# Gated branch of the mixer by pairs of feature tiles, with recurrent gates and scans moved forward

## The chip, the cores and the metric

The kernel runs on one core of a Trainium2 chip. The metric is the device time of one execution in microseconds (us), as a median over runs. The engines are named as in the profile: PE is TensorE's matmul, PEld its weight load, DVE is VectorE, ACT is ScalarE, POOL is GpSimd, SP is SyncE, which issues the loads. Only ACT and DVE take matmul results out of PSUM; POOL works on SBUF alone here.

## The reference, cut to what matters

One layer over 512 tokens of 1024 features: a gated feed-forward net (1024 to 2816 and back), a mixer, and a second feed-forward net, each between root-mean-square norms. The mixer is what the change touches:

```
u = rms_norm(h, mix_pre_g)
q, k, v, xr, xg = split(u @ w_in)              # xr, xg: 1024 features each
xr = causal_conv(xr, conv_w, conv_b)           # 4 taps along the tokens
r  = sigmoid(blockdiag(xr, wa) + ba);  ig = sigmoid(blockdiag(xr, wx) + bx)
a  = exp(-8 r softplus(-lambda));      b  = sqrt(1 - a*a) * ig * xr
hr[t] = a[t]*hr[t-1] + b[t]                    # scan along the tokens
y_a = (hr * gelu(xg)) @ w_lru_out              # the gated branch
y_b = attention(q, k, v) @ w_attn_out
merged = sigmoid(u@wgA + bA) * y_a + sigmoid(u@wgB + bB) * y_b
h = h + rms_norm(merged @ w_o, mix_post_g)
```

All of it is in float32.

## The kernel before

**Split matmuls.** Every operand of a matmul is a pair: `hi`, the value rounded to the fast matmul type, and `lo`, the rest. ACT writes `hi` by a copy and DVE writes `lo` by a subtraction (`split2`, L191, and `split_to`, L151). A product is three matmuls: hi·hi, lo·hi and hi·lo. The activations `u` lie transposed (features on partitions) in `uT`, `hi` and `lo` for 8 feature tiles of 128 by 512 tokens. A *unit* (`unit`, L209; `mm_feat`, L196) makes one output feature tile of 128 by 512 tokens: 8 feature tiles deep, three matmuls of 512 columns each, so 24 matmuls.

**Pairs.** In the feed-forward nets, `Pairs` (L477) makes two output feature tiles at a time by seven block products for eight (the Winograd form of Strassen's method). The weights of two tiles are cut in four blocks, the activations in four blocks of (4 feature tiles) x (256 tokens). Weight sums S1 to S4 and activation sums T1 to T4 are formed first; a product (`mm_s`, L465) is 4 feature tiles deep, three matmuls of 256 columns each, so 12 matmuls, and some of the products accumulate on another's PSUM bank after ACT has copied a partial result out (`q1`, `q5`, `u`, `v`). `prep(m, i)` (L492) prepares the weights of job m in five steps: 0 forms the sums (on POOL in the second net), 1 splits the first raw tile, 2 splits S1 and S2, 3 splits S3 and S4, 4 splits the last block. Its order of products is a11, s1, (a22 of the job before), s2, a12, s4, s3; so ACT's copy of a11's result must come before s2 accumulates on the same bank.

**Order of the work.** The order on each engine is that of the program text; there is no scheduler. `order` (L102 to L132) lists the weight tiles in the order of use, `get` (L163) issues loads and splits a few tiles ahead, and `split_to` stops at tiles that are marked `paired`. `later(n, fn, rank)` (L177) defers work by n *points*; a unit has two points (after each half), a token tile of `wv` and a product of a pair have one. At a point, work that is due is put out in order of rank; `point(True)` puts out all that is left. A deferred step lands in the engines' queues at its point, and an engine that is ahead may do it earlier in time, an engine that is behind later.

**The mixer's projections.** `tok_gemm` (L333) ends the first net: the last 7 feature tiles are taken token tile by token tile, each token tile is normed, transposed by PE into PSUM and copied to `uT` (`transpose_out`, L317). With `xf` given, `transpose_xf` (L327) copies each transposed bank a second time, unrounded, to four tiles of SBUF; the second net's call has that (for T1 to T4 there), the first net's call, L888, has it not. Then come the units, 8 of `xr` (the first four inside `tok_gemm`), 8 of `wg`, 2 of `wk`, 4 token tiles of `wv`, 2 of `wq`, and 8 of `xg`. Counted from the end of `tok_gemm`, `xr` 4 to 7 take points 1 to 8, `wg` 9 to 24, `wk` 25 to 28, `wv` 29 to 32, `wq` 33 to 36, `xg` 37 to 52.

**The recurrent branch** rides along on points: `conv` (L914), `rg_gates` (L924; with `products`, 24 half-height matmuls for two tiles, and `gates`, four tanh on ACT each), `rg_decay` (L965; exp and tanh), `rg_scan` (L978; sqrt on ACT, then after a lag a product and the scan on DVE). The points stand in `CONV_AT`, `RG_AT`, `DECAY_AT`, `SCAN_AT`, `SCAN_LAG` (L1276 to L1284). The scan writes over the tile that held the convolved `xr`, one of 8 that live until `y_out` (L1070), which takes gelu of an `xg` unit, multiplies by the scan and splits the result.

**After it** come the 8 units of `lru` (over the 8 tiles `y`), mixed with the rest of `wq`, `wg` and the steps of attention (L1188 to L1214).

**Slots.** Nearly all SBUF tiles come from one pool of 42 slots of 4 KB per partition (`NSLOT`). A tile's first writer, a load, ACT, DVE or POOL, waits until the last reader of the slot's previous tile is done. PSUM has 8 banks, handled the same way.

Of the kernel before, what the change touches and what calls it, by code (L numbers as in the profile page):

```python
# [51 lines left out]
def hybrid_layer(ctx: ExitStack, tc: tile.TileContext, a: dict, out: bass.AP):  # L52
    nc = tc.nc
    act, dve, pool, pe, sp = nc.scalar, nc.vector, nc.gpsimd, nc.tensor, nc.sync
# [20 lines left out]
    def f32(ap):  # L75
        return ap.bitcast(F32)
# [9 lines left out]
    veps = cp.tile([P, NT], F32, name="veps")  # L86
# [15 lines left out]
    order = []  # L102
# [4 lines left out]
    paired = set()  # L107
# [26 lines left out]
    st = {"dma": 0, "split": 0, "get": 0}  # L134
# [42 lines left out]
    def later(n, fn, rank=1):  # L177
        uid[0] += 1
        due.append((now[0] + n, rank, uid[0], fn))
# [11 lines left out]
    def split2(hi, lo, src):  # L191

        act.activation(hi, src, AF.Copy)  # L193
        dve.tensor_tensor(out=lo, in0=src, in1=f32(hi), op=ALU.subtract)  # L194

    def mm_feat(ps, w, c0=0, c1=SEQ, xh=None, xl=None):  # L196

        wh, wl = w
        for k in range(KT):
            s = slice(k * P, (k + 1) * P)  # L200
            h_ = uT[:, 0, k, c0:c1] if xh is None else xh[k][:, c0:c1]
            l_ = uT[:, 1, k, c0:c1] if xl is None else xl[k][:, c0:c1]
            pe.matmul(ps[:, c0:c1], wh[:, s], h_, start=k == 0, stop=False)  # L203
            pe.matmul(ps[:, c0:c1], wl[:, s], h_, start=False, stop=False)  # L204
            pe.matmul(ps[:, c0:c1], wh[:, s], l_, start=False, stop=k == KT - 1)  # L205
# [231 lines left out]
    class Hidden:  # L437


        def __init__(self):  # L440
            self.f, self.t, self.done = [], {}, 0
# [35 lines left out]
    class Pairs:  # L477

        def __init__(self, na, nb, f0, X, hid, R=None):
            self.R = R
            self.jobs = [(nm, f) for f in range(f0, FT, 2) for nm in (na, nb)]
            self.na, self.X, self.hid = na, X, hid
            self.k0 = order.index((na, f0))
            self.w, self.c1, self.ready = {}, {}, set()

        def raws(self, m):
# [52 lines left out]
        def run(self, tail, hooks={}):  # L541
# [75 lines left out]

            last()

# [43 lines left out]
    hid, X1 = Hidden(), {}  # L663
    hid.f = [None] * NC1
    Rb = slot([P, 2, SEQ], name="Rb")
    pairs_a = Pairs("w1a", "w3a", NC1, X1, hid, Rb)
    h_load([a["x"][t * P : (t + 1) * P, :] for t in range(NT)])
    dma_to(NS + 3)
    dma_one(pairs_a.k0)
# [4 lines left out]
    ps = [bank("f") for _ in range(NS)]  # L674
# [23 lines left out]
    xg, tg = {(hh, th): slot([P, 4, 256], name="xg") for hh in range(2) for th in range(2)}, {}  # L698
# [17 lines left out]
    s4 = small(NT, "s4")  # L716
# [165 lines left out]
    X1 = pairs_a = late = None  # L882
# [4 lines left out]
    bs = tok_gemm("w2a", hid, FT, RF, "ffn1_post_g", 0.5, "mix_pre_g", [("xr", i) for i in range(4)], hid.to, spill=True, eps=veps)  # L887
    hid = None  # L888


# [87 lines left out]
    def rg_scan(i):  # L978
        s0, s1 = lru[i]
        t, ig, a_ = s0[:, 1, :], s1[:, 0, :], s1[:, 1, :]  # L980

        act.activation(t, t, AF.Sqrt, scale=0.25)

        def scan():
            dve.tensor_tensor(out=ig, in0=t, in1=ig, op=ALU.mult)
            dve.tensor_tensor_scan(t, a_, ig, 0.0, op0=ALU.mult, op1=ALU.add)
            lru[i] = s0

        later(SCAN_LAG[i], scan, 3)


    lru = {}
# [19 lines left out]
    for i in range(8):  # L1012
        ps = unit("wg", i)
# [16 lines left out]
    for i in range(2):  # L1030
        ps = unit("wk", i)
# [8 lines left out]
    for t in range(NT):  # L1040
        ps = bank("v")
        c = slice(t * P, (t + 1) * P)
# [21 lines left out]
    for i in range(2):  # L1064
        ps = unit("wq", i)
        later(1, lambda i=i, ps=ps: q_out(i, ps))

    ys = []

    def y_out(i, ps):  # L1070
        t = slot([P, 2, SEQ], name="ge")
        act.activation(t[:, 0, :], ps, AF.Gelu_apprx_tanh)
        dve.tensor_tensor(out=t[:, 1, :], in0=t[:, 0, :], in1=lru.pop(i)[:, 1, :], op=ALU.mult)
        y = slot([P, 2, SEQ], F32R, name="y")
        split2(y[:, 0, :], y[:, 1, :], t[:, 1, :])
        ys.append(y)
# [124 lines left out]
    for nm, i in att_units:  # L1201
        if nm == "lru":
            w = get(nm, i) if i else w_lru
            ps = bank("f")
            mm_feat(ps, w, xh=[y[:, 0, :] for y in ys], xl=[y[:, 1, :] for y in ys])
            later(1, lambda i=i, ps=ps: ya_out(i, ps))
            if i == 7:
                ys.clear()
# [21 lines left out]

    hid, tn = Hidden(), []
    X2 = {"b11": uview(0, 0), "b21": uview(1, 0), "b22": uview(1, 1)}
    pairs_b = Pairs("w1b", "w3b", NC2, X2, hid)
    dma_one(pairs_b.k0)
    dma_one(pairs_b.k0 + 1)
    for i, at_ in enumerate((2, 5, 7, 9, 11)):
# [1 line left out]
    for i in range(8):  # L1238
        if i:
            w = get("wao", i)  # L1240
        ps = bank("f")
# [4 lines left out]
    xf = {(hh, th): slot([P, 4, 256], name="xf") for hh in range(2) for th in range(2)}  # L1246
    def operands():
# [24 lines left out]
    X2 = pairs_b = None  # L1272
# [13 lines left out]
RF = 7  # L1286
RO = 6

NC1 = 4

NG = 2
NC2 = 2
# [54 lines left out]
```

## Time and profile before

| what | value |
|---|---|
| median of 3 runs | 1132.8 us (1132.72 to 1133.06) |
| profiled execution | 1132.6 us, its span 1130.8 us |
| granted TensorE clock | 0.998 |
| PE busy | 1122.6 us (99% of the span) |
| PEld, DVE, ACT, POOL busy | 1006.0, 797.2, 599.5, 303.8 us |
| bytes moved | 124.95 MB, mean 110 GB/s |

The span reaches from the first to the last instruction. A matmul's recorded time is longer than its distance to the next one, since matmuls overlap; the distance from start to start is what one costs. A wait for several things is put down to the one that came last.

### The profile page before, as it was taken

Reading aid. Unit: us, or ns where it says so; the run is one execution under the profiler, and the core shown is the slowest. Engines: PE = TensorE matmul, PEld = TensorE weight load, DVE = VectorE, ACT = ScalarE, POOL = GpSimd, SP = SyncE. Lnnn points to the kernel's source line nnn. Section 1 sums busy time; section 2 is a strip of 40 time slices with the busy share of each in tenths; the row PEclk is TensorE's granted clock in tenths of the full one; section 3 lists DMA queues with packets and bytes.
Section 4 is the critical chain, followed back from the end, with each engine's and each line's share of the span. In section 5 each row is a group of like instructions: output and inputs, shape, how many; then the busy total and the mean of one; then the engine's idle time right before and its main releaser. Section 6 shows DMA issues by size and latency. Waiting matters only on the chain.

```text
span 1130.8 us, 17501 instructions
## 1 busy us (share of the span) xinstructions
PE 1122.6 (99%) x6829; PEld 1006.0 (89%) x6829; DVE 797.2 (70%) x1219; ACT 599.5 (53%) x1065; POOL 303.8 (27%) x243
## 2 busy tenths in 40 slices
PE   9999999999999999999999999999999999999997
PEld 7899999988889887888888888889999999998886
DVE  5889989886446747695778855667898777975313
ACT  7755555574335359844656653356555555573211
POOL 0044444200000000001655642000965566700000
PEclk9999999999999999999999999999999999999999
DMA  9226563265314312134232333521332332254101
GB/s 343 88 95 148 133 131 112 76 223 168 102 59 152 119 54 71 60 111 132 60 90 76 94 118 99 184 104 39 112 95 94 112 112 79 90 199 173 39 19 56
DMA packets 37138, 124.95 MB, mean 110 GB/s; under 512 B 4528, under 2 KB 6448, under 8 KB 37056
## 3 DMA queue, kind: packets, MB, share of 16 engines
q1 hardware_dynamic: 34128, 114.89, 30.2%
q0 software_dynamic: 2640, 8.43, 3.7%
q8 instruction: 53, 0.87, 0.3%
q10 hardware_dynamic: 288, 0.52, 0.1%
q14 instruction: 29, 0.24, 0.1%
HBM read 116.50 MB, written 7.33 MB: 110 GB/s over the span
## 4 chain that ended last, share of the span: by engine, by line
PE 97%; ACT 2%; DVE 1%; issue 0%; DVEq 0%
PE c L472 11%; PE c L473 11%; PE c L474 11%; PE f L203 10%; PE f L204 10%; PE f L205 10%; PE acc L223 8%; PE acc L221 8%; PE acc L222 8%; PE pt L1148 1%; PE s L1112 1%; PE s L1111 1%; PE tr L313 1%; PE o L1164 1%; PE o L1165 1%; PE f L693 1%
## 5 line engine op out<-in xcount | busy, mean ns | idle before, releaser
L203 PE MATMUL f<-uT,whi 128*128 128x512 f32 (+1 forms) x472 | 171.6, 364 | 0.0
L204 PE MATMUL f<-uT,wlo 128*128 128x512 f32 (+1 forms) x472 | 170.3, 361 | 0.1
L205 PE MATMUL f<-uT,whi 128*128 128x512 f32 (+1 forms) x472 | 170.1, 360 | 0.0
L221 PE MATMUL acc<-whi,hT 128*128 128x512 f32 x352 | 137.1, 390 | 0.0
L222 PE MATMUL acc<-wlo,hT 128*128 128x512 f32 x352 | 137.0, 389 | 0.0
L223 PE MATMUL acc<-whi,hT 128*128 128x512 f32 x352 | 136.9, 389 | 0.0
L472 PE MATMUL c<-Xh,whi 128*128 128x256 f32 x456 | 129.1, 283 | 0.0
L474 PE MATMUL c<-Xl,whi 128*128 128x256 f32 x456 | 129.1, 283 | 0.0
L473 PE MATMUL c<-uT,wlo 128*128 128x256 f32 x456 | 129.0, 283 | 0.0
L473 PE MATMUL c<-Xh,wlo 128*128 128x256 f32 x456 | 129.0, 283 | 0.0
L474 PE MATMUL c<-uT,whi 128*128 128x256 f32 x456 | 129.0, 283 | 0.0
L472 PE MATMUL c<-uT,whi 128*128 128x256 f32 x456 | 129.0, 283 | 0.0
L194 DVE TENSOR_TENSOR wlo<-S,whi 128x1024 fp32r<-128x1024 f32 x76 | 113.7, 1496 | 2.0 <-ACT whi L193 1.1
L203 PEld LDWEIGHTS f<-uT,whi 128*128 128x128 f32 x472 | 89.1, 189 | 14.5 <-issue 1.4
L204 PEld LDWEIGHTS f<-uT,wlo 128*128 128x128 f32 x472 | 89.2, 189 | 13.5 <-DVE wlo L159 0.5
L205 PEld LDWEIGHTS f<-uT,whi 128*128 128x128 f32 x472 | 89.1, 189 | 13.5
L193 ACT ACTIVATE whi<-S 128x1024 fp32r<-128x1024 f32 x76 | 77.9, 1055 | 19.8 <-DVE S L518 19.8
L472 PEld LDWEIGHTS c<-Xh,whi 128*128 128x128 f32 x456 | 87.5, 192 | 0.3 <-issue 0.3
L472 PEld LDWEIGHTS c<-uT,whi 128*128 128x128 f32 x456 | 87.5, 192 | 0.0
L473 PEld LDWEIGHTS c<-uT,wlo 128*128 128x128 f32 x456 | 87.5, 192 | 0.0
L474 PEld LDWEIGHTS c<-uT,whi 128*128 128x128 f32 x456 | 87.5, 192 | 0.0
L473 PEld LDWEIGHTS c<-Xh,wlo 128*128 128x128 f32 x456 | 87.5, 192 | 0.0
(324 smaller groups left out, 2705.2 us busy)
## 6 DMA issues: line engine op xcount, KB each, us to landing
raw_w2a<-in_w2a_dram SPq DMA_DIRECT2D x22, 512.0 KB, 4.3
raw_w1b<-in_w1b_dram SPq DMA_DIRECT2D x22, 512.0 KB, 4.2
raw_w3b<-in_w3b_dram SPq DMA_DIRECT2D x22, 512.0 KB, 4.1
raw_w2b<-in_w2b_dram SPq DMA_DIRECT2D x22, 512.0 KB, 4.2
raw_w3a<-in_w3a_dram SPq DMA_DIRECT2D x21, 512.0 KB, 4.5
raw_w1a<-in_w1a_dram SPq DMA_DIRECT2D x20, 512.0 KB, 4.3
raw_wg<-in_wg_dram SPq DMA_DIRECT2D x16, 512.0 KB, 3.8
raw_xr<-in_xr_dram SPq DMA_DIRECT2D x8, 512.0 KB, 4.0
```

The costliest lines, as they stand in the source:

```text
L193: act.activation(hi, src, AF.Copy)
L194: dve.tensor_tensor(out=lo, in0=src, in1=f32(hi), op=ALU.subtract)
L203: pe.matmul(ps[:, c0:c1], wh[:, s], h_, start=k == 0, stop=False)
L204: pe.matmul(ps[:, c0:c1], wl[:, s], h_, start=False, stop=False)
L205: pe.matmul(ps[:, c0:c1], wh[:, s], l_, start=False, stop=k == KT - 1)
L221: pe.matmul(acc[n], x[:, 0, c], wh[:, s], start=first, stop=False)
L222: pe.matmul(acc[n], x[:, 0, c], wl[:, s], start=False, stop=False)
L223: pe.matmul(acc[n], x[:, 1, c], wh[:, s], start=False, stop=last)
L313: pe.transpose(ps[:, k * P : (k + 1) * P], hg[:, kk * P : (kk + 1) * P], ident)
L472: pe.matmul(ps, wh[:, s], xh, start=first, stop=False, skip_group_check=True)
L473: pe.matmul(ps, wl[:, s], xh, start=False, stop=False, skip_group_check=True)
L474: pe.matmul(ps, wh[:, s], xl, start=False, stop=k == 3, skip_group_check=True)
```

## The change

The eight `xg` units are replaced by four jobs of a new class `GeluPairs`, derived from `Pairs` (whose constructor now takes the names and an end). Each job makes two feature tiles by seven products of 12 matmuls; gelu, the product with the scan (`mult`) and the split of the result (`parts`) are done for two tiles at once, one job later. The last job's are done at the end, in pieces.

The activation sums T1 to T4 are needed for the mixer's `u` now: `xf` is given to the first net's `tok_gemm`, POOL does four subtractions in place on these tiles, and each is split to two slots at points 4, 5, 7 and 9 (`T_AT`). The first job's weight sums and splits are put at points 27, 30, 32, 33 and 34 (`PREP_AT`), the second job's sums, on POOL, at 34. The `xg` tiles are marked `paired`, so that `split_to` leaves them alone.

Gates move from points 7 to 23 to points 4 to 18, decays from 15 to 28 to points 10 to 23, the square roots from 29 to 32 to points 26 to 29, and the lags of the scans shrink, so that the last scan stands at point 34 and not 42. The scans write to four tiles of their own (two scans in each).

```diff
@@ order
+    paired.update(range(len(order), len(order) + 8))
     order += [("xg", i) for i in range(8)]
@@ after class Pairs
+    class GeluPairs(Pairs):
+        def run(self, scans, yh, yl, tail):
...
+            for n, (nm, f) in enumerate(self.jobs):
+                W = self.w.pop(n)
+                tmp = slot([P, 4, 256], name="ct")
+                q1, q5, u, v = (tmp[:, i, :] for i in range(4))
+                c = slot([P, 2, SEQ], name="cc")
+                bu, bx, bc = (bank("c")[:, :256] for _ in range(3))
+                mm_s(W["a11"], X["b11"], bu)
+                act.activation(q1, bu, AF.Copy)
+                mm_s(W["s1"], X["t1"], bx)
+                act.activation(q5, bx, AF.Copy)
+                self.prep(n + 1, 1)
+                last()
+                mm_s(W["s2"], X["t2"], bu, True)
+                act.activation(u, bu, AF.Copy)
+                mult()
+                self.prep(n + 1, 2)
+                mm_s(W["a12"], X["b21"], bc)
+                dve.tensor_tensor(out=c[:, 0, :256], in0=bc, in1=q1, op=ALU.add)
+                mm_s(W["s4"], X["b22"], bx, True)
+                dve.tensor_tensor(out=c[:, 0, 256:], in0=bx, in1=u, op=ALU.add)
+                parts()
+                self.prep(n + 1, 3)
+                if n == end:
+                    tail()
+                mm_s(W["s3"], X["t3"], bu, True)
+                act.activation(v, bu, AF.Copy)
+                dve.tensor_tensor(out=c[:, 1, 256:], in0=v, in1=q5, op=ALU.add)
+                gelu(c[:, 0, :])
+                if n < end:
+                    self.prep(n + 1, 4)
+                    self.prep(n + 2, 0)
+                self.raws(n + 3)
+                def last(W=W, bu=bu, c=c):
+                    mm_s(W["a22"], X["t4"], bu, True)
+                    act.activation(c[:, 1, :256], bu, AF.Gelu_apprx_tanh)
+                    gelu(c[:, 1, 256:])
+                def mult(c=c, sc=scans[f // 2]):
+                    dve.tensor_tensor(out=c, in0=c, in1=sc, op=ALU.mult)
+                def parts(c=c):
+                    yh.append(slot([P, 2, SEQ], F32R, name="yh"))
+                    yl.append(slot([P, 2, SEQ], F32R, name="yl"))
+                    split2(yh[-1], yl[-1], c)
+            # after the loop: mult, gelu and split of the last job in pieces, tail(), its a22
...
@@ first net's tok_gemm
+    xf = {(hh, th): slot([P, 4, 256], name="xf") for hh in range(2) for th in range(2)}
-    bs = tok_gemm("w2a", hid, FT, RF, ..., hid.to, spill=True, eps=veps)
+    bs = tok_gemm("w2a", hid, FT, RF, ..., hid.to, xf=xf, spill=True, eps=veps)
@@ rg_scan
-            dve.tensor_tensor_scan(t, a_, ig, 0.0, op0=ALU.mult, op1=ALU.add)
-            lru[i] = s0
+            if i % 2 == 0:
+                scans.append(slot([P, 2, SEQ], name="scan"))
+            dve.tensor_tensor_scan(scans[i // 2][:, i % 2, :], a_, ig, 0.0, op0=ALU.mult, op1=ALU.add)
@@ before the laters of conv, gates, decays, scans
+    pairs_g = GeluPairs(("xg",), 0, 8, X3)
+    for o_, p_, q_ in (((0, 0), (0, 1), (0, 0)), ((0, 1), (1, 1), (0, 1)), ((1, 1), (1, 1), (0, 0)), ((1, 0), (1, 0), (1, 1))):
+        pool.tensor_tensor(out=xf[o_], in0=xf[p_], in1=xf[q_], op=ALU.subtract)
+    for n, (key, o_) in enumerate((("t1", (0, 0)), ("t3", (0, 1)), ("t2", (1, 1)), ("t4", (1, 0)))):
+        later(T_AT[n], lambda key=key, o_=o_: X3.update({key: to_slots(xf.pop(o_))}), 3)
+    for i, p in enumerate(PREP_AT):
+        later(p, lambda i=i: pairs_g.prep(0, i), 3)
+    later(PREP_AT[-1], lambda: pairs_g.prep(1, 0), 3)
@@ after the units of wq
-    for i in range(8):
-        ps = unit("xg", i)
-        later(1, lambda i=i, ps=ps: y_out(i, ps))
+    yh, yl = [], []
+    point(True)
+    pairs_g.run(scans, yh, yl, lambda: split_to(st["split"] + 1))
@@ constants
-RG_AT = (7, 11, 13, 15, 17, 19, 21, 23)
+RG_AT = (4, 6, 8, 10, 12, 14, 16, 18)
-DECAY_AT = (15, 16, 19, 20, 23, 24, 27, 28)
-SCAN_AT = (29, 29, 30, 30, 31, 31, 32, 32)
-SCAN_LAG = (1, 2, 2, 4, 5, 7, 8, 10)
+DECAY_AT = (10, 11, 14, 15, 18, 19, 22, 23)
+SCAN_AT = (26, 26, 27, 27, 28, 28, 29, 29)
+SCAN_LAG = (1, 2, 2, 3, 3, 4, 4, 5)
+T_AT = (4, 5, 7, 9)
+PREP_AT = (27, 30, 32, 33, 34)
```

More of the change, by code (lines that the diff above doesn't have):

```diff
@@ L618, in run @@
             last()
+    class GeluPairs(Pairs):
+        def run(self, scans, yh, yl, tail):
+            X, end = self.X, len(self.jobs) - 1
+            assert st["get"] == st["split"] == self.k0, (st, self.k0)
+            st["get"] = st["split"] = self.k0 + 2 * len(self.jobs)
+            last = mult = parts = lambda: None
+            gelu = lambda v: act.activation(v, v, AF.Gelu_apprx_tanh)
+            for n, (nm, f) in enumerate(self.jobs):
[40 more added lines that the diff above has]
+                    split2(yh[-1], yl[-1], c)
+            sc, h_, l_ = scans[-1], slot([P, 2, SEQ], F32R, name="yh"), slot([P, 2, SEQ], F32R, name="yl")
+            dve.tensor_tensor(out=c[:, 0, :], in0=c[:, 0, :], in1=sc[:, 0, :], op=ALU.mult)
+            gelu(c[:, 1, 256:])
+            dve.tensor_tensor(out=c[:, 1, 256:], in0=c[:, 1, 256:], in1=sc[:, 1, 256:], op=ALU.mult)
+            split2(h_[:, 0, :], l_[:, 0, :], c[:, 0, :])
+            tail()
+            mm_s(W["a22"], X["t4"], bu, True)
+            act.activation(c[:, 1, :256], bu, AF.Gelu_apprx_tanh)
+            dve.tensor_tensor(out=c[:, 1, :256], in0=c[:, 1, :256], in1=sc[:, 1, :256], op=ALU.mult)
+            split2(h_[:, 1, :], l_[:, 1, :], c[:, 1, :])
+            yh.append(h_)
+            yl.append(l_)
@@ L886, in hybrid_layer @@
     later(10, softplus)
-    bs = tok_gemm("w2a", hid, FT, RF, "ffn1_post_g", 0.5, "mix_pre_g", [("xr", i) for i in range(4)], hid.to, spill=True, eps=veps)
+    xf = {(hh, th): slot([P, 4, 256], name="xf") for hh in range(2) for th in range(2)}
+    bs = tok_gemm(
+        "w2a", hid, FT, RF, "ffn1_post_g", 0.5, "mix_pre_g", [("xr", i) for i in range(4)], hid.to, xf=xf, spill=True, eps=veps)
     hid = None
@@ L1066, in hybrid_layer @@
         later(1, lambda i=i, ps=ps: q_out(i, ps))
[L1068 to L1076, printed above, removed]
-    for i in range(8):
-        ps = unit("xg", i)
-        later(1, lambda i=i, ps=ps: y_out(i, ps))
+    yh, yl = [], []
+    point(True)
+    pairs_g.run(scans, yh, yl, lambda: split_to(st["split"] + 1))
+    X3 = pairs_g = None
     def ya_out(i, ps):
```

19 lines of the change are left out of this document (9 added, 10 removed).

## The prediction

> **What bounds the kernel now.** I read the page's busy times first, then the chain of work that ended last, then PE's own rows where the change sits.
>
> ```profile
> PE 1122.6 (99%) x6829; PEld 1006.0 (89%) x6829; DVE 797.2 (70%) x1219; ACT 599.5 (53%) x1065; POOL 303.8 (27%) x243
> PE 97%; ACT 2%; DVE 1%; issue 0%; DVEq 0%
> 478.38 0.39 PE L205 MATMUL f<-uT,whi 128*128 128x512 f32 x1
> 483.82 0.39 PE L205 MATMUL f<-uT,whi 128*128 128x512 f32 x1
> 484.73 0.39 PE L203 MATMUL f<-uT,whi 128*128 128x512 f32 x1
> 485.19 0.50 PE L204 MATMUL f<-uT,wlo 128*128 128x512 f32 x1
> 528.61 0.39 PE L203 MATMUL f<-y,whi 128*128 128x512 f32 x1
> 82.87 0.28 PE L472 MATMUL c<-Xh,w 128*128 128x256 f32 x1
> 84.31 0.28 PE L472 MATMUL c<-Xh,whi 128*128 128x256 f32 x1
> ```
>
> PE is 97% of the chain, so time is won only by fewer or cheaper matmuls, and lost wherever PE comes to wait. The two rows at 478.38 and 483.82 are 24 matmuls apart: 226.7 ns each at 512 columns. Those at 82.87 and 84.31 are 12 apart, one product of a pair: 120.0 ns each at 256 columns. A line through both is 13.3 ns per matmul plus 0.417 ns per column, so halving a matmul doesn't halve its cost. The eight `xg` units begin at 484.73 and the first `lru` matmul is at 528.61: 43.88 us, of which 192 x 0.2267 = 43.52 is matmuls; most of the other 0.36 is the wait before 485.19 (0.23 beyond the usual distance).
>
> The gain rests on ACT and DVE keeping up, so next comes the busy time by stretch (PE, PEld, DVE, ACT, POOL, clock, DMA).
>
> ```profile
> 326.00:376.00 50.00, 50.00 (x317) 45.32 (x317) 36.37 (x74) 24.18 (x54) 2.77 (x4) 1.00 0.40 147
> 752.00:802.00 50.00, 50.00 (x326) 45.70 (x326) 36.86 (x72) 31.00 (x67) 10.69 (x5) 1.00 0.13 43
> 380.00:390.00 10.00, 10.00 (x45) 8.26 (x44) 6.00 (x8) 1.60 (x3) 0.00 (x0) 1.00 0.19 54
> 430.00:440.00 10.00, 10.00 (x46) 8.05 (x46) 6.70 (x11) 9.78 (x14) 0.00 (x0) 1.00 0.26 86
> 470.00:480.00 10.00, 10.00 (x62) 8.93 (x61) 7.21 (x12) 9.07 (x18) 0.00 (x0) 1.00 0.17 52
> 485.00:529.00 44.00, 43.93 (x194) 36.30 (x194) 33.16 (x39) 18.32 (x26) 4.87 (x10) 1.00 0.42 132
> 820.00:1000.00 180.00, 180.00 (x1502) 180.00 (x1501) 145.21 (x153) 96.40 (x171) 108.14 (x64) 1.00 0.31 101
> ```
>
> ACT is nearly full from 430 to 480 and idle before 390. The last row is the second net's pairs: 180 us at PE 180.00, with POOL forming the weight sums and DVE at 81%.
>
> **The change, part by part.**
>
> *PE.* Removed: 192 x 0.2267 = 43.52 us plus the 0.36. Added: 4 jobs x 7 products x 12 = 336 matmuls x 0.1200 = 40.32. Net -3.56 us if PE never waits. An eighth of 43.52 would be 5.44; the 144 extra matmuls take 1.92 of it back (144 x 13.3 ns).
>
> [...]
>
> *Second copies in the first net's `tok_gemm`, sums T on POOL, their splits.* Prices:
>
> ```profile
> L330 ACT ACTIVATE xf<-tr x8: 578/609/649, 767.9 to 790.4; 128x512 f32<-128x512 f32 x8
> L1251 DVE TENSOR_TENSOR T<-xf,xf x1: 1224/1224/1224, 790.6 to 790.6; 128x1024 f32<-128x1024 f32 x1
> L1253 DVE TENSOR_TENSOR T<-xf,T x1: 2311/2311/2311, 795.1 to 795.1; 128x1024 f32<-128x1024 f32 x1
> 791.16 2.95 POOL L1255 TENSOR_TENSOR T<-xf,xf 128x1024 f32<-128x1024 f32 x1 [49.65 <-ACT xf L330]
> 800.90 2.28 POOL L518 TENSOR_TENSOR S<-raw_w3b,raw_w3b 128x512 f32<-128x512 f32 x1
> 906.85 1.92 DVE L194 TENSOR_TENSOR wlo<-raw_w3b,whi 128x1024 fp32r<-128x1024 f32 x1
> 366.32 2.36 DVE L159 TENSOR_TENSOR wlo<-raw_xr,whi 128x1024 fp32r<-128x1024 f32 x2
> ```
>
> Eight copies x 0.61 = 4.9 us of ACT, four behind the last transposes (2.4 us). The second net's call runs with them (752 to 802) at PE 50.00 and ACT 31.0; the first's stage has ACT at 24.2. Cost 0; without that cover 2.4. Then 4 x 2.95 = 11.8 us of POOL, from about 367 to 379. A DVE subtraction of two SBUF tiles takes 1.22 us alone and 2.31 beside POOL's sum (L1251, L1253), so the four subtractions from 366.32 on end some 4 us later, before 375; the first weights are wanted at 378.9. Cost 0. Four splits at points 4 to 9, 4 x 1.05 of ACT and 4 x 1.22 of DVE, fall into the stretch with ACT at 1.6 of 10. The last one stands ahead of `conv(7)`, which feeds the gates' products at point 12: I count about 0.5 us to spare there, so 0 to 0.5 of waiting; 0 taken, since three of the four splits are long done.
>
> *Gates, decays, roots.* The same instructions, earlier. PE's 24 half-height matmuls per pair of tiles stay; ACT's full stretch (one round of 12.7 us: 8 tanh, 4 of the decays, 2 gates, 2 splits) starts four or five points sooner. Cost 0 by itself; what it buys is ACT time before the pairs: its work after the last decay (eight roots, `wk` and `wv` outputs, splits, `wq`) adds up to about 25 us, an estimate, with 31 to do it in.
>
> *DVE up to the second job.* This is the tight place. Rows:
>
> ```profile
> L986 DVE TENSOR_TENSOR_SCAN xc_t<-ig_e x8: 1224/1224/1226, 478.4 to 504.7; 128x512 f32<-128x512 f32 x8
> L985 DVE TENSOR_TENSOR ig_e<-xc_t,ig_e 128x512 f32<-128x512 f32 x8 | 5.5, 685 | 0.0
> L1061 DVE SCALAR_TENSOR_TENSOR QS<-f,QS 64x512 fp32r<-64x512 f32 x16 | 11.0, 688 | 0.5 <-ACT QS L1059 0.3
> 452.50 0.42 PE r L956
> 458.35 0.68 ACT ig_e L940
> 464.55 0.82 ACT ig_e L968
> 462.45 0.69 DVE KS L1024
> 477.39 0.43 DVE V L194
> 476.44 0.43 DVE L974 TENSOR_SCALAR ig_e<-ig_e 128x512 f32<-128x512 f32 x1
> 504.72 1.23 DVE L986 TENSOR_TENSOR_SCAN xc_t<-ig_e 128x512 f32<-128x512 f32 x1
> 483.93 1.21 DVE wlo L159
> ```
>
> Today the last scan ends at 506, 21 us into the `xg` units; the change queues all eight ahead of the pairs. The last gates' products go from 452.5 to about 439 (5 points of 2.72), their tanh end at 445 instead of 459, and after two decays of 1.64, two splits and two gates on ACT the last factors on DVE end at about 454 instead of 477 (an estimate). From there DVE owes, before the second job's first weights are whole: 8 scans x 1.91 = 15.3; `lo` of `wv` and `wq` 4.9; `wk`, `wv` and `wq` outputs 2.8 + 1.7 + 2.8; first job's preparation 3 x 1.22 + 0.68 = 4.3; the second's first `lo` 1.2. Sum 33.0, so 487. Beside it POOL forms 8 weight sums of up to 2.28 (17 to 18 us), and next to POOL such a subtraction takes 1.92 rather than 1.22 (906.85): up to 6.5 us lost, which gives 493.5; waits on `wk` and `wv` can add 2. The second job starts six products after 484.73, at 493.4. So 0 to 2.1 us of waiting. I take 0.5: the last row shows the present stage already entering with a DVE backlog of this kind, and PE lost only about 0.3 to it.
>
> *Inside the jobs.* In the second net a job of 10.08 us costs DVE 8.1 (145.21 over 17.9 jobs) and ACT 5.4. Here the multiplication by the scan and the residual of two tiles, 1.22 each as L1251, come on top, and the second net's own product and silu (about 1 and 0.7 us a job) go, for gelu and a split on ACT (1.4 + 1.05): DVE about 9.6, ACT about 7.2, estimates. That holds for two of the four jobs; the first has nothing to multiply, the last nothing to prepare. ACT's copy of a11's result must be done 1.44 us later in the first job (2.88 later on); ACT enters idle by my count. Gelu waits for DVE's sums and stands ahead of that copy, so a DVE more than 1.5 us later than above would be felt a second time. 0 taken.
>
> *Exit.* After the last product ACT and DVE owe the last two tiles some 6 us (gelu, multiplication, two splits, two splits of `lru` and `wq` weights); the seventh and eighth tile are wanted 4.1 us after the end plus 0.9 of attention scores, that is 6.4 after s3. Cost 0 to 1; 0 taken. Step 0 of attention starts about 2 us later on DVE and has room:
>
> ```profile
> 537.21 3.17 POOL L1132 TENSOR_SCALAR P<-P,d 128x128 f32<-128x128 f32 x4 [7.42 <-ACT es L1126]
> 545.10 0.60 PE L1148 MATMUL pt<-ident,P 128*128 128x128 f32 x4
> ```
>
> POOL is done at 540.4 and PE asks at 545.1.
>
> *Loads.* The same bytes, no new ones; the `xg` loads sit at the same place of SP's queue, apart from tiles 2 and 3, now behind the slots that the scans free.
>
> *Sum.* -3.56 + 0.5 = -3.1 on the profiled 1132.6, so 1129.5; the median stands 0.2 above that execution: **1129.7 us**.
>
> **The rivals.**
>
> *The gain is eaten at the entry (no change).* The DVE backlog or a late copy stops PE for 1.3 to 5.8 us in the first two jobs. For it: the sum above ends within 0.1 us of its deadline at POOL's full interference. Against it: PE 180.00 of 180 in the second net with the same interference. Time 1130.5 to 1135.1.
>
> *Slots starve the second job (slower).* By the program text, point 27 has all 42 slots taken (4 `wg`, 2 of `wk`, 8 of T, 16 of the recurrent branch, 6 split weights, 4 raw tiles, 2 sums), while the stage today holds about 31 there. The raw tiles of the second job then wait for the scans:
>
> ```profile
> SPq L143 <- DVE xc_t L986: 25.2, 4, 9.9
> DMA to landing us min/median/max: 3.4/3.7/4.4
> 518.19 2.18 POOL L1093 DMA_DIRECT2D BT<-bias_scr  x4 [163.86 <-PE f L205]
> ```
>
> Four of SP's loads already wait for scans, and POOL's load for attention waits for a slot until 518. If the last raw tile is issued at 489, it lands at 493, S1 and S2 take POOL 4.5, the split 3: 500, wanted at 494.8, and ACT, held at S3 and S4, delays the copies PE waits for. That is 5 to 9 us, so 1134 to 1138. It decides when that tile lands after about 493.3: then the stop passes 5.8 us, which is 3.56 plus 0.2% of the time. Against it: a scan every 2 us frees two slots.
>
> [...]
>
> *A full eighth.* If 256 columns cost half of 512, 1127.5. The rows at 82.87 and 84.31 exclude it.
>
> **How the numbers follow.** 0.2% (2.3 us) is about what a measurement of this kernel can tell from no change. Gain mostly kept, 1129.0 to 1130.5: 0.52, the forecast. Eaten at the entry: 0.28. Slots 0.17 and exclusion 0.02: slower, 0.19 together. Full eighth 0.01, below the range. The gain is little above the bound, so faster is 0.53 only, same 0.28, slower 0.19. The range runs from 1129.0 (no wait at all is 1129.2, less the spread) to 1136.0, which leaves out the upper part of the slot rival (0.10), exclusion and the full eighth. The likeliest case's own range is 1129.0 to 1130.5.
>
> **What the new profile would show.** Right: PE rows of `c` at 120 ns from about 484.7, the first `lru` matmul 40.3 to 41 us later, no idle PE above 0.3 us before 484.7; the last scan on DVE before 490; DVE about full from 455 to 515. Wrong: PE waiting for `wlo` at the second job (entry), SP's load of `xg` 2 or 3 after 488 or POOL's sums of the second job ending after 497 (slots), DVE subtractions of 3 us and more (exclusion), PE waiting at the gates' products or at the first `xr` units (the moved steps), or on `yl` in `lru` (exit).

## The result, and the profile after

| kernel | median | against the kernel before (95% interval) | span of the profiled execution |
|---|---|---|---|
| before | 1132.74 us | | 1130.8 us |
| changed | 1140.97 us | 1.0076 [1.0063, 1.0089] | 1138.8 us |

Each kernel ran six times: 1132.6 to 1133.1 us before, 1140.5 to 1142.7 us changed. The change makes the kernel 8.2 us slower; the forecast was 3.1 us faster. In the two traces the whole difference lies in the branch's own stage. From its first matmul to the first one of `lru` it took 43.88 us; now the stage goes from 484.38 to 536.38, 52.00 us, although its matmuls are 336 x 0.120 = 40.32. So PE stood still or ran slowly for 11.7 us.

The changed kernel's page (first line and busy times), then PE's rows behind its waits, in order of time (start, duration, line, operation; in brackets the idle time and what ended it):

```profile
span 1138.8 us, 17875 instructions
PE 1122.6 (99%) x6973; PEld 1012.7 (89%) x6973; DVE 831.6 (73%) x1238; ACT 618.9 (54%) x1102; POOL 345.2 (30%) x263
```

```profile
487.13 0.28 PE L475 MATMUL c<-Xl,whi 128*128 128x256 f32 x1
490.79 0.58 PE L473 MATMUL c<-Xh,whi 128*128 128x256 f32 x1 [3.38 <-ACT ct L637]
...
499.05 0.39 PE L474 MATMUL c<-uT,wlo 128*128 128x256 f32 x1 [0.68 <-DVE wlo L195]
...
513.37 0.39 PE L474 MATMUL c<-Xh,wlo 128*128 128x256 f32 x1 [2.54 <-DVE wlo L195]
...
518.29 0.39 PE L473 MATMUL c<-Xh,whi 128*128 128x256 f32 x1 [0.60 <-ACT ct L637]
...
534.85 0.38 PE L473 MATMUL c<-Xh,w 128*128 128x256 f32 x1 [0.47 <-ACT ct L655]
```

Measured from start to start beyond the usual 0.12, the five waits are 3.54, 0.83, 2.70, 0.90 and 0.63 us: ACT's copy `q1` of the first job, the first weights of the second, S1 of the third, `q1` of the third, and ACT's copy `v` ahead of the last product. That is 8.6. Another 2.7 are two stretches of matmuls at about 0.21 us instead of 0.12, from 490.8 and from 514.7 on (the first is shown at the end of this document), and 0.4 are slower first matmuls after a wait (0.22 or 0.23 us to the next). Before 484 PE waits nowhere, as forecast.

The busy time by stretch (PE, PEld, DVE, ACT, POOL, each with its number of instructions, then granted clock, DMA share, GB/s) shows who was late:

```profile
440.00:460.00 20.00, 20.00 (x90) 16.52 (x89) 10.31 (x14) 17.16 (x25) 0.00 (x0) 1.00 0.34 106
460.00:470.00 10.00, 10.00 (x78) 9.65 (x77) 9.90 (x7) 5.96 (x10) 6.71 (x4) 1.00 0.10 16
480.00:490.00 10.00, 7.41 (x45) 6.42 (x43) 9.93 (x9) 4.06 (x6) 6.18 (x4) 1.00 0.20 55
490.00:500.00 10.00, 8.54 (x57) 8.34 (x58) 9.76 (x11) 5.69 (x8) 1.38 (x1) 0.83 0.00 2
```

DVE is full from 480 to 500 and half idle from 440 to 460. ACT, named at the longest wait, is busy 4.06 of 10 there. Its own rows tell what held it:

```profile
486.51 1.20 ACT L1143 ACTIVATE QS<-f 64x512 fp32r<-64x512 f32 x2 [3.71 <-DVE scan L1060]
488.68 1.20 ACT L1143 ACTIVATE QS<-f 64x512 fp32r<-64x512 f32 x2 [0.97 <-DVE wlo L195]
490.35 0.38 ACT L637 ACTIVATE ct<-c 128x256 f32<-128x256 f32 x1 [0.47 <-DVE ig_e L1057]
```

Three instructions in a row need a fresh slot (`QS`, `QS`, `ct`), and each waits until DVE has let one go: by a scan, by a split, by the product ahead of a scan. The `q1` copy that PE asks for stands behind them. So the question becomes why DVE is late. Two things are in its rows. First its idle time, while scans whose square roots were done (the first two at 454.4, inside the first of these gaps) stood behind other work in its queue:

```profile
455.40 1.23 DVE L160 TENSOR_TENSOR wlo<-raw_wv,whi 128x1024 fp32r<-128x1024 f32 x1 [1.64 <-ACT whi L159]
459.15 1.41 DVE L1108 TENSOR_TENSOR KS<-f,KS 64x512 fp32r<-64x512 f32 x2 [2.53 <-ACT KS L1106]
...
471.79 1.41 DVE L1108 TENSOR_TENSOR KS<-f,KS 64x512 fp32r<-64x512 f32 x2 [1.33 <-ACT KS L1106]
474.31 0.42 DVE L195 TENSOR_TENSOR V<-v,V 128x256 fp32r<-128x256 f32 x1 [1.10 <-ACT V L194]
```

These four are 6.6 us. Second its instructions beside POOL's weight sums, here those of the second job (DVE, then POOL):

```profile
484.22 2.20 DVE L1060 TENSOR_TENSOR_SCAN scan<-ig_e 128x512 f32<-128x512 f32 x1
486.34 2.24 DVE L195 TENSOR_TENSOR wlo<-S,whi 128x1024 fp32r<-128x1024 f32 x1
488.51 1.75 DVE L1057 TENSOR_TENSOR ig_e<-xc_t,ig_e 128x512 f32<-128x512 f32 x1
490.36 2.10 DVE L1060 TENSOR_TENSOR_SCAN scan<-ig_e 128x512 f32<-128x512 f32 x1
```

```profile
460.26 1.29 POOL L523 TENSOR_TENSOR S<-raw_xg 128x512 f32<-128x512 f32 x1 [81.26 <-DVE KS L1108]
...
483.67 1.67 POOL L523 TENSOR_TENSOR S<-raw_xg 128x512 f32<-128x512 f32 x1 [16.54 <-DVE wlo L195]
485.42 2.09 POOL L524 TENSOR_TENSOR S<-S,raw_xg 128x512 f32<-128x512 f32 x1
487.58 2.12 POOL L518 TENSOR_TENSOR S<-raw_xg,S 128x512 f32<-128x512 f32 x1
489.67 1.71 POOL L519 TENSOR_TENSOR S<-raw_xg,raw_xg 128x512 f32<-128x512 f32 x1
```

The four DVE instructions take 8.29 us where they take 4.3 elsewhere in this trace or in that of before (scan and split 1.22 each, product 0.68). With the first job's sums, from 460 on, DVE loses 7.8 us to eight sums, about 1 us a sum. And POOL's sums themselves came late for want of slots: the second raw tile of the first job could be issued only at 456.48, when a matmul had let its slot go, and landed 3.6 us later, just ahead of the sum at 460.26. (The 81 us in that row are POOL's idle time, in which it had no other work.)

The third job's raw tiles had the same fate (SP, POOL, DVE):

```profile
499.06 1.28 SPq L144 DMA_DIRECT2D raw_xg<-in_xg_dram  x3
504.00 2.15 POOL L523 TENSOR_TENSOR S<-raw_xg 128x512 f32<-128x512 f32 x1 [12.61 <-DMA raw_xg<-in_xg_dram]
...
511.03 2.28 DVE L195 TENSOR_TENSOR wlo<-S,whi 128x1024 fp32r<-128x1024 f32 x1 [3.80 <-POOL S L519]
```

They could be issued only when DVE had split the second job's first raw tile (497.77 to 499.00), which stands behind the last scan in its queue; they landed near 504, and the split of S1 and S2 was done at 513.3, when PE had been asking for it since 510.7.

Two theories came out of this. SLOTS: the 42 slots are full, and ACT, POOL and SP wait for what only DVE's scans release. CONTENTION: POOL's sums slow DVE's instructions of two SBUF inputs (a scan takes up to 2.20 us for 1.22). A third way to see it, BACKLOG, is that DVE's queue has the scans in a place where they end too late.

### The profile page after: what moved, and what is told of

It reads as the page before. It is cut to its first block, busy times and chain, and to the rows that moved or that the text cites. A ratio compares the mean times of both kernels' runs of the same rounds, so it can differ in the third digit from the quotient of the medians.

```text
span 1138.8 us, 17875 instructions
## 1 busy us (share of the span) xinstructions
PE 1122.6 (99%) x6973; PEld 1012.7 (89%) x6973; DVE 831.6 (73%) x1238; ACT 618.9 (54%) x1102; POOL 345.2 (30%) x263
## 4 chain that ended last, share of the span: by engine, by line
PE 54%; DVE 0%; issue 0%; ACT 0%; DVEq 0%; ACTq 0%
PE c L473 6%; PE c L474 6%; PE c L475 6%; PE f L204 5%; PE f L206 5%; PE f L205 5%; PE acc L224 5%; PE acc L222 5%; PE acc L223 5%; PE pt L1223 1%; PE s L1187 1%; PE s L1186 1%; PE o L1239 1%; PE o L1240 1%; PE tr L314 0%
## 5 line engine op out<-in xcount | busy, mean ns | idle before, releaser
L473 PE MATMUL c<-Xh,whi 128*128 128x256 f32 x504 | 143.5, 285 | 4.0 <-ACT ct L637 4.0
L204 PE MATMUL f<-uT,whi 128*128 128x512 f32 (+1 forms) x408 | 146.7, 360 | 0.0
L474 PE MATMUL c<-Xh,wlo 128*128 128x256 f32 x504 | 143.3, 284 | 2.5 <-DVE wlo L195 2.5
L205 PE MATMUL f<-uT,wlo 128*128 128x512 f32 (+1 forms) x408 | 145.3, 356 | 0.0
L206 PE MATMUL f<-uT,whi 128*128 128x512 f32 (+1 forms) x408 | 145.2, 356 | 0.0
L474 PE MATMUL c<-uT,wlo 128*128 128x256 f32 x504 | 142.9, 283 | 0.7 <-DVE wlo L195 0.7
L475 PE MATMUL c<-Xl,whi 128*128 128x256 f32 x504 | 143.3, 284 | 0.0
L473 PE MATMUL c<-uT,whi 128*128 128x256 f32 x504 | 142.7, 283 | 0.0
L475 PE MATMUL c<-uT,whi 128*128 128x256 f32 x504 | 142.7, 283 | 0.0
L475 PEld LDWEIGHTS c<-Xl,whi 128*128 128x128 f32 x504 | 97.4, 193 | 0.0
L473 PEld LDWEIGHTS c<-uT,whi 128*128 128x128 f32 x504 | 97.0, 192 | 0.1
L475 PEld LDWEIGHTS c<-uT,whi 128*128 128x128 f32 x504 | 96.9, 192 | 0.0
L204 PEld LDWEIGHTS f<-uT,whi 128*128 128x128 f32 x408 | 77.1, 189 | 12.0 <-issue 1.1
L206 PEld LDWEIGHTS f<-uT,whi 128*128 128x128 f32 x408 | 77.1, 189 | 11.0
```

Source lines behind the costliest of these rows:

```text
L473: pe.matmul(ps, wh[:, s], xh, start=first, stop=False, skip_group_check=True)
L474: pe.matmul(ps, wl[:, s], xh, start=False, stop=False, skip_group_check=True)
L475: pe.matmul(ps, wh[:, s], xl, start=False, stop=k == 3, skip_group_check=True)
```

## The experiments

The runs stand in three groups (e1, e2, e3, f1; e4, e5, f2, f3; e6, f5, f6, f7), each with its own runs of the kernel before, whose medians are 1132.33, 1132.48 and 1132.51 us against the 1132.74 above. A difference between two groups is good to some 0.4 us, and the 95% interval of a ratio is about 1 us to either side; where less than that is read off, the stage in the traces has to bear it out.

**Four slots fewer for T2 and T4 (e1).**

```diff
-    def to_slots(src):
+    def to_slots(src, p=None):
-        p = slot(..., name="Xh"), slot(..., name="Xl")
+        p = p or (slot(..., name="Xh"), slot(..., name="Xl"))
...
+        over = {"t2": "t1", "t4": "t3"}.get(key)      # the slots of T1 and T3
```

> Changed kernel, with the split parts of T2 and T4 written into the slots of T1 and T3 (the same instructions, four of the 42 slots fewer; the products of T2 and T4 so read the wrong factor or parts of it, which leaves the time of each instruction as it was). Theory SLOTS (the eight scans, ScalarE's copies, the loads of tiles 4 to 7 and GpSimd's sums stand behind slots that only VectorE's scans release, and this makes the 8.9 us of TensorE waits in the jobs): with four slots free the loads of tiles 4 to 7 are issued some 10 us earlier and most of the waits go, 1130 to 1133 us. Theory CONTENTION (GpSimd's sums make VectorE's multiplies and scans 1.7 to 2.3 us instead of 0.7 to 1.2, and VectorE so ends late): the sums are the same and lie beside the same scans, 1138 to 1141 us.

Measured: 1133.58 us, 1.0012 [1.0003, 1.0021], so 7.4 us of the loss gone. The loads of tiles 4 to 7 are issued from 484.78 and not 499.06, and the 3.5 us wait in the first job is gone, since ACT gets its slots in time (`q1` is copied at 486.40). Besides the 0.63 us at the end of the last job, one wait is left, for the second job's first weights, and 1.7 us of matmuls at half speed behind it (PE, then POOL's first sum):

```profile
495.44 0.39 PE L474 MATMUL c<-uT,wlo 128*128 128x256 f32 x1 [1.76 <-DVE wlo L195]
...
453.22 2.10 POOL L523 TENSOR_TENSOR S<-raw_xg 128x512 f32<-128x512 f32 x1 [73.83 <-DVE ig_e L1050]
```

The expectation had the sums beside the same scans, and that didn't hold: with slots to be had, the first job's sums begin at 453.22 and not 460.26, and the first two scans are back at 1.23 us. The second job's sums still lie beside the scans (two scans of 2.20 us at 480.5 and 486.7). So this run frees slots and takes away half of the contention at once; it doesn't part the two theories.

**Constants for POOL's sums (e2).**

```diff
                 e = eng or pool
+                if self.na == "xg":
+                    e.tensor_tensor(out=s12[:, :1], in0=a21[:, :1], in1=a11[:, :1], op=ALU.add)
+                    e.memset(s12[:, 1:], 0.5)
+                    e.memset(s34, 0.5)
+                    return
```

> Changed kernel, with GpSimd's sums of weight tiles for the four jobs replaced: one column of one sum, the rest filled with a constant, so GpSimd reads almost nothing from SBUF but writes the same tiles in the same slots at the same place (this leaves the sums out, and TensorE multiplies by constants in their place). Theory CONTENTION: VectorE's scans stay at 1.22 us and its multiplies at 0.68 us, the last scan ends by 488 us, 1130 to 1133 us. Theory SLOTS: the slots are held as long as before, the loads of tiles 4 to 7 come within 2 us of where they came, 1136 to 1140 us.

Measured: 1129.92 us, 0.9977 [0.9968, 0.9986]: 11.0 us below the changed kernel with not one slot more. All scans are back at 1.22, and PE's only wait of note is the one at the end of the last job (the scans' group, with duration min/median/max in ns; a DVE and a POOL row at the same time and the second job's first split; PE's wait):

```profile
L1065 DVE TENSOR_TENSOR_SCAN scan<-ig_e x8: 1224/1225/1227, 461.7 to 488.3; 128x512 f32<-128x512 f32 x8
```

```profile
461.72 1.23 DVE L1065 TENSOR_TENSOR_SCAN scan<-ig_e 128x512 f32<-128x512 f32 x1
461.82 0.95 POOL L526 MEMSET S<- 128x1024 f32 x1
...
492.41 1.23 DVE L195 TENSOR_TENSOR wlo<-raw_xg,whi 128x1024 fp32r<-128x1024 f32 x1
```

```profile
PE c L473 <- ACT ct L660: 0.5, 1, 0.5
```

This is the forecast's case without interference, and the time is near the forecast's 1129.7: -3.56 for the matmuls, +0.73 at the end of the last job and +0.27 at the second one's first weights make -2.56, and the spans differ by 2.6. The loads of tiles 4 to 7 are issued at 493.7, 5 us earlier than in the changed kernel, just because the scans end earlier. So the slots and the slower DVE instructions are one chain: a slot is free when a scan is done, and a scan is late when sums lie beside it. Removing either link takes away most of the loss. The run also makes POOL's part of a job shorter (2.0 us for the first job, 6.9 in the changed kernel); DVE's rows show the contention gone, and e4 below takes the sums off POOL in another way.

Two things in the traces narrow down what slows which instructions. The scan at 461.72 took 1.23 us beside a memset, which writes SBUF and has no input; beside the changed kernel's sums four scans took 2.10 to 2.20. And in the second net of the changed kernel, where POOL forms the weight sums too, DVE's additions of 128x256 from PSUM and SBUF (`cc<-c,ct`, L580) stay at 405 to 420 ns, beside a sum or not, while those of two SBUF inputs (`cc<-ct`, L592) take 0.41 or 0.42 us without a sum and 1.51 or 1.52 wholly beside one. In the changed kernel's rows from 483.67 to 492.46, four sums (1.29 us alone, as the one at 508.46 with DVE idle) and four DVE instructions (4.3) would make 9.5 us one after the other, and took 8.8.

**The moved gates, decays and scans alone, in the kernel before (e3).**

```diff
-RG_AT = (7, 11, 13, 15, 17, 19, 21, 23)
+RG_AT = (4, 6, 8, 10, 12, 14, 16, 18)
...
-SCAN_AT = (29, 29, 30, 30, 31, 31, 32, 32)
+SCAN_AT = (26, 26, 27, 27, 28, 28, 29, 29)
```

> Kernel before with one part of the change alone: recurrent gates, decays and scans at the changed kernel's points, the branch still by eight block products. Both theories (the move itself costs nothing, the loss is in the pairs): 1132 to 1133.5 us, no change. Rival MOVE (the scans at points 26 to 29 push VectorE's work ahead of the xg units late by themselves): 1135 us or more.

Measured: 1132.43 us, 1.0003 [0.9994, 1.0012]. No change, as expected: the move costs nothing and brings nothing by itself.

**The pairs alone, gates and scans back in their old places (e6).** The same lines of constants the other way round, in the changed kernel (the short lags kept).

> Changed kernel with the other part undone: gates, decays and scans back at the points of the kernel before (only the lags that shorten the last scans kept), the branch by pairs. Theory BACKLOG (what the pairs cost is that VectorE's scans end after the first products, so the scans' place decides): the scans start some 15 us later and hold their slots as long, TensorE waits longer ahead of the first two jobs than the 8.9 us of the changed kernel: 1146 to 1156 us. Rival (the move of the scans is what hurt): below 1140 us.

Measured: 1151.51 us, 1.0167 [1.0154, 1.0181]. PE's waits in that stage:

```profile
PE c L473 <- ACT ct L637: 11.4, 3, 9.3
PE c L474 <- DVE wlo L195: 4.9, 3, 2.1
```

Now the copy `q1` is 9.3 us late in one place. The place of the recurrent steps (gates, decays and scans, moved together here) decides what the pairs cost: 10.5 us between this run and the changed kernel, some 1 us of it half-speed matmuls. It is the reason why the move belongs to the change, and a hint that moving further pays.

**Fewer slots by sharing in the recurrent branch (f1).** The input gates of two tiles share a slot, the decay is written over the convolved input, the scan over its own input.

```diff
-        s1 = slot([P, 2, SEQ], name="ig_e")
-        lru[i] = (s0, s1)
+        if i % 2 == 0:
+            scans.append(slot([P, 2, SEQ], name="ig"))
...
-            dve.tensor_tensor_scan(scans[i // 2][:, i % 2, :], a_, ig, 0.0, op0=ALU.mult, op1=ALU.add)
+            dve.tensor_tensor_scan(ig, a_, ig, 0.0, op0=ALU.mult, op1=ALU.add)
```

> Changed kernel with four slots fewer held up to the scans: the input gates of two feature tiles share a slot, the decay is written over the convolved input, and the scan is written over its own input; same instructions at the same points. Theory SLOTS: like the run with T2 and T4 in the slots of T1 and T3, 1129.5 to 1133 us, so faster than the kernel before or the same. Theory CONTENTION: 1138 to 1141 us.

Measured: 1138.71 us, 1.0057 [1.0045, 1.0070]. This missed SLOTS, but it isn't CONTENTION that made it: its scans run as in e1. By the program text the sharing saves four slots before the scans and none after them (each scanned pair now frees two slots where it freed three on balance), and the loads of tiles 4 to 7 came at 495.26, against 484.78 in e1. The second job's wait is that of e1 (1.91 us), and the third job has two more, of 2.81 and 2.09 us:

```profile
507.34 2.27 DVE L195 TENSOR_TENSOR wlo<-S,whi 128x1024 fp32r<-128x1024 f32 x1 [3.80 <-POOL S L519]
```

Its sums end at 507.3, where e1's ended at 498.7. As far as these two runs show, what counts is slots at the time of the last scans, not the number saved before.

**Sums on DVE (e4).**

```diff
-                e = eng or pool
+                e = eng or (dve if self.na == "xg" else pool)
```

> Changed kernel, with the sums of the four xg jobs on VectorE instead of GpSimd, at the same places of the program (everything else, slots included, as it was). VectorE gets four 128x512 sums of 0.68 us per job, 2.7 us more, and loses what GpSimd's sums cost it (about 8 us over the first two jobs). Theory CONTENTION as the one that decides, with slots as what makes it worse: most of the gain of the run with constant sums (11 us against the changed kernel) comes back, less 2.7 us of VectorE's work for each of the first two jobs: 1131 to 1136 us. Theory SLOTS alone: the slots go as before, and VectorE ends no earlier: 1139 us or more.

Measured: 1134.64 us, 1.0018 [1.0009, 1.0027]: 6.3 us gained. The scans take 1.22 us, DVE pays 4 x 0.69 a job for the sums, and besides the 0.63 us at the end of the last job one wait is left, with DVE late at the second job (3.33 us from start to start, and 1.5 us of half speed behind it):

```profile
L1060 DVE TENSOR_TENSOR_SCAN scan<-ig_e x8: 1224/1224/1225, 464.3 to 491.5; 128x512 f32<-128x512 f32 x8
```

```profile
496.86 0.39 PE L474 MATMUL c<-uT,wlo 128*128 128x256 f32 x1 [3.18 <-DVE wlo L195]
```

So DVE is better off doing a 0.69 us sum than sharing its time with POOL's.

**One slot more (e5).** The room comes from a padding tile.

```diff
-    cp.tile([P, 168], F32, name="gap")
+    cp.tile([P, 160], F32, name="gap")
...
-NSLOT = 42
+NSLOT = 43
```

> Changed kernel with 43 slots instead of 42, the room taken from padding. Theory SLOTS AND CONTENTION TOGETHER (the missing slots push GpSimd's sums of the first job from 453 us, where VectorE is half idle, to 460 us, where it scans): with one more slot the first job's sums start by 455 us if one slot was what they lacked, the first two scans go back to 1.22 us, and the time falls by 2 to 5 us, to 1136 to 1139 us. CONTENTION ALONE, wherever the sums lie: no change, 1140 to 1142 us.

Measured: 1135.04 us, 1.0023 [1.0014, 1.0032]: 5.9 us gained by one slot, more than expected. The sums of the first job start at 458.11, not by 455, and only one of the first two scans got its 1.22 us back; but ACT's copy `q1` comes at 486.34 instead of 490.35, and the long wait of the first job is gone. DVE is still late: PE waits 3.06 us for the second job's first weights. All waits of the stage make 4.9 us against 8.6, and the changed kernel's 2.7 us of half-speed matmuls are gone too (POOL, then PE):

```profile
458.11 1.29 POOL L523 TENSOR_TENSOR S<-raw_xg 128x512 f32<-128x512 f32 x1 [78.81 <-DMA raw_xg<-in_xg_dram]
...
496.51 0.38 PE L474 MATMUL c<-uT,wlo 128*128 128x256 f32 x1 [2.89 <-DVE wlo L195]
```

**43 slots and earlier scans (f2).**

```diff
-SCAN_AT = (26, 26, 27, 27, 28, 28, 29, 29)
-SCAN_LAG = (1, 2, 2, 3, 3, 4, 4, 5)
+SCAN_AT = (26, 26, 26, 26, 27, 27, 28, 28)
+SCAN_LAG = (0, 0, 1, 1, 1, 1, 1, 2)
```

> Changed kernel with 43 slots and the scans earlier in the order (the first two at the point of their square roots, the rest one or more points earlier), so that VectorE scans in its idle 454 to 460 us and the slots come free some 4 us earlier. Both theories expect a gain over the run with 43 slots alone; with contention left in the second job's sums, 1131 to 1136 us; if slots alone decide, 1129.5 to 1131 us.

Measured: 1131.38 us, 0.9992 [0.9983, 1.0001]: 3.7 us below the run with 43 slots alone and near the kernel before. Two scans now fill DVE's idle time:

```profile
454.52 0.69 DVE L1057 TENSOR_TENSOR ig_e<-xc_t,ig_e 128x512 f32<-128x512 f32 x1 [0.17 <-ACT xc_t L1054]
455.31 1.23 DVE L1060 TENSOR_TENSOR_SCAN scan<-ig_e 128x512 f32<-128x512 f32 x1
```

The last scan begins at 482.4 (493.7 in the changed kernel). This is BACKLOG shown, with one slot more: with the same work for DVE and the same sums on POOL, the order is worth 3.7 us (3.5 in the stage, and neither trace has half-speed matmuls). Two scans are slow beside sums in either run. `SCAN_AT` also moves six of the square roots on ACT up a point, which the run doesn't part from DVE's order, and no run moved the scans alone with 42 slots.

**The second job's sums on DVE as well (f3), then those of the third and fourth (f5).**

```diff
-                e = eng or pool
+                e = eng or (dve if self.na == "xg" and m == 1 else pool)     # f3
+                e = eng or (dve if self.na == "xg" and m > 0 else pool)      # f5
```

> As the run with 43 slots and earlier scans, and the second job's sums on VectorE (2.7 us of its own instead of about 3.4 us of slower scans and multiplies beside GpSimd). Theory CONTENTION: 1 to 2 us below that run, 1129.5 to 1133 us. Theory SLOTS: the same as that run or slower by up to 2.7 us.

> As the run with 43 slots, earlier scans and the second job's sums on VectorE, with the sums of jobs 3 and 4 there too (only the first job's stay on GpSimd). Theory CONTENTION: the 0.6 us wait at 515 us goes, since 2.7 us of VectorE's own replaces some 4 us of slower instructions a job: 1130.0 to 1130.8 us. Against it: no gain, 1130.8 to 1132 us, if VectorE's time there is no shorter for it.

Measured: 1130.83 us, 0.9985 [0.9976, 0.9994], and 1130.35 us, 0.9980 [0.9971, 0.9989]. Each step brings half a microsecond, f3 less than the 1 to 2 that I expected. That is within the intervals; the stage bears it out, with 42.17 us in f2, 41.76 in f3 and 41.04 in f5. f5 beats both kernels: 2.2 us below the one before, 10.6 below the changed one. PE waits once in its stage:

```profile
524.28 0.38 PE L473 MATMUL c<-Xh,w 128*128 128x256 f32 x1 [0.47 <-ACT ct L655]
```

**s3 and s4 exchanged in the last job (f6), and the same with POOL's sums for jobs 3 and 4 (f7).**

```diff
                 dve.tensor_tensor(out=c[:, 0, :256], in0=bc, in1=q1, op=ALU.add)
+                if n == end:
+                    mm_s(W["s3"], X["t3"], bu, True)
+                    act.activation(v, bu, AF.Copy)
                 mm_s(W["s4"], X["b22"], bx, True)
```

> As the run with all sums but the first job's on VectorE, and in the last job the products s3 and s4 exchanged, so that ScalarE's copy out of the bank of s3 lies beside s4 instead of ahead of a22. The 0.64 us wait at the end of the last job, which stands in every run with pairs, goes: 0.5 to 0.7 us below that run, 1129.3 to 1130.3 us. If the wait comes back at the exit (the last tile's multiply and split later than the final product's other operands), no change.

> As the run before this, but with GpSimd's sums for jobs 3 and 4 (VectorE has the second job's alone). CONTENTION: 0.3 to 1 us above the run with all but the first on VectorE, 1130 to 1130.6 us; without it the same.

Measured: 1131.10 us, 0.9987 [0.9978, 0.9996], and 1131.63 us, 0.9992 [0.9983, 1.0001]. Both are above what I expected. The wait at the last product goes, and f6's stage takes 40.31 us, exactly its matmuls. But DVE's sum behind s4, and with it the split of `lru`'s weights, comes 1.45 us later, and PE waits for those instead (f6; 1.35 us from start to start):

```profile
526.68 0.50 PE L205 MATMUL f<-yh,wlo 128*128 128x512 f32 x1 [1.19 <-DVE wlo L160]
```

So 0.63 us were exchanged for 1.35, and f5 stays the best. f7 stands 0.5 us above f6, and its stage has one wait of 0.60 us for DVE in the last job; it is the price of POOL's sums for the last two jobs once more.

## Why the prediction was wrong

*PE's -3.56 us: right.* In f5 the stage takes 41.04 us, 40.31 beside the wait at its end, against a forecast of 40.32.

*Second copies, sums and splits of T, moved gates and decays at no cost: right.* PE waits nowhere from 340 to 484 in the changed kernel, and the move alone gives 1.0003. But the four DVE subtractions beside POOL's sums T, forecast to end some 4 us later and before 375, end at 380.1. They take 12.2 us, and 4.8 in the kernel before, yet PE does not wait for them (POOL's four sums, then the last of DVE's four):

```profile
366.54 12.45 POOL L1068 TENSOR_TENSOR xf<-xf,xf 128x1024 f32<-128x1024 f32 x4 [11.82 <-ACT xf L331]
376.66 3.42 DVE L160 TENSOR_TENSOR wlo<-raw_xr,whi 128x1024 fp32r<-128x1024 f32 x1
```

*DVE up to the second job: this step failed.* Its start (454 forecast, 452.6 in the trace), its work (33.0 us; e2 shows 41.0 us from 452.6 to the end of the second job's first `lo` at 493.6, less 8.5 of idle time, so 32.5) and the interference (6.5 forecast, 7.8 measured) were all near. The term that was wrong is the one priced in half a sentence, "waits on `wk` and `wv` can add 2", and then left at nothing in the taken value: DVE's queue idled 6.6 us here, 8.5 in e2, because finished square roots had their scans placed behind work that waited for ACT. With it the second job's first weights are whole at 499.0 and not 493.5. Either loss alone just fits: e2 has the idle time and no interference, and they are whole at 493.6; f2 has interference (scans of 2.2 us) and 1.5 us of idle time, and they are whole at 492.6. The forecast had room for one of the two. f2 shows that the idle time was to be had by order, there with one slot more.

*Inside the jobs, 0 taken: wrong by consequence.* "ACT enters idle by my count" was true of ACT's work and false of its queue: it had nothing to do, and stood behind three slots. The sentence that a DVE more than 1.5 us late "would be felt a second time" was right, though gelu was not the way; it came first, by slots, in the first job (3.54 us).

*The rival of the slots: right in kind, wrong in place.* It was priced on the second job's raw tiles, and neither of the signs named for it came: these were issued at 468.24 and 479.18, and POOL's sums of them ended at 491.4. The slots stopped ACT at `QS` and the loads of the third job, at 499. Its size, 5 to 9 us, was short of the 11.7 us lost. The argument against it, "a scan every 2 us frees two slots", assumed scans on time.

*Exclusion, given 0.02: not shown.* The name stands for POOL and DVE shutting each other out. Its sign, DVE subtractions of 3 us and more, came true beside the sums T (the 3.42 us above, for 1.22), where one of POOL's sums took 3.1. But beside the weight sums DVE's scans, splits and products took 0.8 to 1.1 us longer, less than one sum alone (1.29), and POOL's sums, all but the first, 1.63 to 2.12. Over the first two jobs DVE lost 7.8 us to eight sums, about 1 us a sum, where the eight took POOL 14.3; its idle time and the slots made up the rest of the loss. No run tells by what the two hold each other up.

*Exit, 0 to 1, 0 taken: 0.73 with the slower first matmul, by another cause.* PE did not wait for `yl` but for ACT's copy out of the bank that the last product accumulates on. The prediction had read that hazard for `q1` and not for `v` of the last job, where nothing stands between s3 and a22.

*Not foreseen: the clock*, below.

## What to carry to other kernels

A queue that is full in one stretch and half idle in the one before has to be added up in order of its queue, with each wait, and not by work; its idle time was the largest error of the sum here. Where a pool of buffers is full, a half idle engine can still be late (ACT here, busy 4.06 of 10 us): ask what releases the next buffer, at that moment. And a sum moved to GpSimd wasn't free for VectorE here: among its instructions of two SBUF inputs eight sums cost it 7.8 us, about 1 us each, more than the 0.69 us in which VectorE did one itself (e4).

## What was not expected of the hardware

After some waits PE came back at half speed (in the changed kernel at 490.8: granted clock 0.50, matmuls 0.21 us apart for 0.12), or fell to it a little later (there at 514.6, 1.2 us behind the wait that ended at 513.4). Stretches of three kernels (columns as above, the clock third from the right), first the changed kernel around its wait of 3.5 us, then e5 behind one of 3.06, then e1 behind one of 1.92:

```profile
490.70:494.10 3.40, 3.31 (x15) 3.31 (x16) 3.37 (x4) 1.71 (x5) 0.68 (x1) 0.50 0.00 0
494.10:497.50 3.40, 3.40 (x31) 3.40 (x30) 3.33 (x5) 1.96 (x3) 0.00 (x0) 1.00 0.01 5
```

```profile
496.60:500.00 3.40, 3.40 (x29) 3.40 (x30) 3.37 (x6) 1.59 (x5) 0.00 (x0) 1.00 0.59 182
```

```profile
495.50:499.50 4.00, 4.00 (x20) 3.85 (x21) 3.97 (x4) 1.08 (x3) 3.24 (x2) 0.58 0.75 242
```

The two of the changed kernel cost 1.56 and 1.1 us on top of the waits. By the traces such stretches cost 3.9 us in e6, 1.7 in e1 and 1.5 in e4 and f1, and nothing in e2, e5, f2, f3, f5, f6 and f7 (the granted clock of the whole execution is 0.991 in e6, 0.997 in the other three and 0.998 or 0.999 in the rest); so differences between runs of the two kinds hold this much that is no wait. The length of the wait doesn't decide alone: 1.92 us set it off in e1, 3.06 in e5 did not. What decides in a given case stays open; no run was made for it.
